# Value half of the last up projection as seven block products for 16 channel tiles

## The chip, the core and the metric

The kernel runs on one core of a Trainium2 chip. What counts is the device time of one execution in microseconds (us). The engines are TensorE (PE), VectorE (DVE), ScalarE (ACT), GpSimd (POOL) and the DMA queues, which SyncE (SP) and ScalarE issue here. SBUF is the on-chip memory, PSUM the accumulators of TensorE, HBM the memory outside.

## The reference

Two layers of an encoder over 256 tokens, width 2048, with 16 learned tokens put in front and dropped at the end:

```python
h = RMSNorm(x)
[q | k | v | f | ga | gf] = h @ W_in
a = attention(q, k, v) @ W_attn_br      # 8 heads, 2 key heads, RMSNorm and rotary on q and k
s = fourier(f) @ W_four                 # Re of a 2-D DFT per channel group
x = x + (sigmoid(ga) * a + sigmoid(gf) * s) @ W_out
h2 = RMSNorm(x)
u = dwconv3(h2 @ W_up_gate)             # taps over positions t-1, t, t+1
x = x + (silu(u) * (h2 @ W_up_val)) @ W_down
```

All is float32. W_up has 2 x 5632 columns: 44 channel tiles of 128 for the gate half and 44 for the value half. The tokens that count in the last layer's value half are 256, two halves of 128.

## The kernel before

**Precision by splitting.** A float32 product is made of three faster ones: each operand is a sum of a high part (a cast to F32R) and a low part (what the cast left), and hi x hi, hi x lo and lo x hi are added in PSUM. Activations are kept so in xHL. Weights come in chunks of 128 x 1024 floats (512 KB): load_raw has SyncE load a chunk (tile raw, four buffers), split_w has ScalarE cast it (wh, line 233, three buffers) and VectorE subtract (wl, line 236). A chunk is 4 k-tiles for 2 channel tiles (MG = 2), and a product over 2048 inputs for two channel tiles is a group of four chunks.

**The order of the work.** The list order, written at the start, names every group and its chunks: mix of a layer (k, v, q, then per half ga, gf, s, a and eight o groups), then the up and down groups. advance keeps loads ahead of use, and the splitting of a chunk is put into the queues LOOK = 2 chunks ahead of its matmuls. Engines take their instructions in the order in which the program issues them. Everything that isn't a weight's split or a matmul hangs between matmuls: generators are pushed with a delay onto a list (shadow), and step(), called after every second k-tile and channel tile, lets one of them go on; drain() runs all that are left at once. A second list (behindhand) holds generators with steps of their own. Folded weights for the Fourier group (fold_w, line 219) use the tile wpm, two buffers, instead of a split.

**Seven products.** In the last layer the down projection of the first 36 channel tiles is made by a scheme with seven block products in place of eight (PRODUCTS): inputs and weights are taken as 2 x 2 blocks, each product multiplies a sum of input blocks by a sum of weight blocks, and results are added into four output blocks (C4). weight_sums makes the four sums of weight blocks needed, on VectorE in layer 0's feed-forward stage, with loads and stores on ScalarE's queue, and stores them in HBM (tsum); later they come as chunks like any weight. The products of one up block's channels run in between the next up block's groups (FF_SPLIT gives the blocks of 22, 14 and 8 channel tiles); combos makes the sums of inputs, block_ the matmuls (line 1043), 512 wide.

**The last up projection.** For each pair of channel tiles a gate group (ug, three matmuls of 258 columns per k-tile and channel tile) is followed by a value group (uv). In the value groups one matmul of 512 columns takes the high weight against both parts of x, and one of 256 the low weight (lines 303, 304). On the gate u is scaled by rstdB, which holds 1/rms for every token, then come the taps (lines 1105, 1107, 1108) and Silu (1109); the product with rstdB (1110) and with the value gives g. The first part of norm_stats (1/rms) is made while the first gate group runs, and drain() is called after that group.

## Time and profile before

| what | us |
|---|---|
| time, median of 3 runs (lowest to highest) | 2509.56 (2509.33 to 2509.77) |
| the profiled execution | 2509.57 |
| its span, from the first to the last instruction | 2507.6 |
| TensorE busy | 2500.3 |
| VectorE busy | 1800.7 |
| ScalarE busy | 1255.1 |
| GpSimd busy | 18.2 |

A row of the groups gives the line, the engine, the operation with the tiles that it writes and reads, shapes and count; then the busy time and the mean in ns of one; then how long the engine was idle just before these instructions, and what ended that wait. A row of the timeline is the start, the length, and the same names, with a wait ahead of it in brackets.

### The profile page before, as it was taken

How to read it: one execution, taken by the hardware profiler on the slowest of the kernel's cores; microseconds unless marked ns; L12 is line 12 of the kernel's file. 1: busy time of each engine (PE TensorE's matmuls, PEld its weight loads, DVE VectorE, ACT ScalarE, POOL GpSimd, SP SyncE). 2: the span in 40 equal slices, each digit the busy share in tenths (PEclk: the TensorE clock that was granted, in tenths of full speed). 3: DMA queues.
4: the chain of work that ended last, by engine and by line, in shares of the span. 5: the costliest groups of instructions: out<-in, count | busy, mean ns of one | idle time of the engine just before them, and what ended most of it. 6: DMA issues, size and time to landing. Idle time of an engine off the chain costs nothing.

```text
span 2507.6 us, 47695 instructions
## 1 busy us (share of the span) xinstructions
PE 2500.3 (100%) x19334; PEld 2432.0 (97%) x19334; DVE 1800.7 (72%) x2717; ACT 1255.1 (50%) x1862; POOL 18.2 (1%) x37
## 2 busy tenths in 40 slices
PE   9999999999999999999999999999999999999999
PEld 9999999999999999999999999999999998888888
DVE  7687666777777557777655887666766668888986
ACT  6455334454454334544444564444544556666663
POOL 0000000000000000000000000000000000000000
PEclk9999999999999999999999999999999999999999
DMA  7545555568888888888754546565555567888885
GB/s 241 167 157 173 184 186 198 178 205 297 281 295 291 286 297 287 288 294 289 252 177 155 178 157 206 188 203 195 192 187 192 187 220 266 267 265 267 268 268 192
DMA packets 160524, 569.15 MB, mean 227 GB/s; under 512 B 18480, under 2 KB 22320, under 8 KB 160304
## 3 DMA queue, kind: packets, MB, share of 16 engines
q1 hardware_dynamic: 135200, 485.69, 58.0%
q10 hardware_dynamic: 25104, 80.43, 9.3%
q8 instruction: 151, 2.47, 0.4%
q14 instruction: 69, 0.57, 0.1%
HBM read 523.41 MB, written 39.85 MB: 225 GB/s over the span
## 4 chain that ended last, share of the span: by engine, by line
PE 98%; DVE 1%; DMA 0%; ACT 0%; issue 0%; SPq 0%; ACTq 0%; DVEq 0%
PE ps_x L1043 7%; PE ps_ug L307 7%; PE ps_ug L309 7%; PE ps_ug L308 7%; PE ps_uv L303 6%; PE ps_d L309 4%; PE ps_d L307 4%; PE ps_d L308 3%; PE ps_uv L307 3%; PE ps_uv L309 3%; PE ps_uv L308 3%; PE ps_uv L304 3%; PE ps_o L307 2%; PE ps_gf L307 2%; PE ps_gf L309 2%; PE ps_s L339 2%
## 5 line engine op out<-in xcount | busy, mean ns | idle before, releaser
L236 DVE TENSOR_TENSOR wl<-raw,wh 128x1024 fp32r<-128x1024 f32 (+1 forms) x889 | 1083.2, 1220 | 555.4 <-ACT wh L233 550.5
L233 ACT CAST wh<-raw 128x1024 fp32r<-128x1024 f32 (+1 forms) x888 | 928.9, 1046 | 929.9 <-PE ps_ug L308 212.7
L307 PE MATMUL ps_ug<-xHL,wh 128*128 128x272 f32 (+1 forms) x1408 | 398.8, 283 | 0.0
L309 PE MATMUL ps_ug<-xHL,wl 128*128 128x272 f32 (+1 forms) x1408 | 397.1, 282 | 0.0
L308 PE MATMUL ps_ug<-xHL,wh 128*128 128x272 f32 (+1 forms) x1408 | 396.8, 282 | 0.0
L307 PEld LDWEIGHTS ps_ug<-xHL,wh 128*128 128x128 f32 x1408 | 264.3, 188 | 2.2
L308 PEld LDWEIGHTS ps_ug<-xHL,wh 128*128 128x128 f32 x1408 | 264.6, 188 | 1.9
L309 PEld LDWEIGHTS ps_ug<-xHL,wl 128*128 128x128 f32 x1408 | 264.4, 188 | 0.0
L303 PE MATMUL ps_uv<-xHL,wh 128*128 128x512 f32 x704 | 247.1, 391 | 0.0
L307 PE MATMUL ps_d<-gHL,wh 128*128 128x272 f32 (+1 forms) x720 | 205.8, 286 | 0.0
L309 PE MATMUL ps_d<-gHL,wl 128*128 128x272 f32 (+1 forms) x720 | 205.2, 285 | 0.0
L308 PE MATMUL ps_d<-gHL,wh 128*128 128x272 f32 (+1 forms) x720 | 204.4, 284 | 0.0
L307 PE MATMUL ps_uv<-xHL,wh 128*128 128x272 f32 x704 | 201.3, 286 | 0.0
L309 PE MATMUL ps_uv<-xHL,wl 128*128 128x272 f32 x704 | 200.6, 285 | 0.0
L308 PE MATMUL ps_uv<-xHL,wh 128*128 128x272 f32 x704 | 199.9, 284 | 0.0
L304 PE MATMUL ps_uv<-xHL,wl 128*128 128x256 f32 x704 | 198.2, 282 | 0.0
L1043 PE MATMUL ps_x<-wh,cb 128*128 128x512 f32 x504 | 171.0, 392 | 0.0
L303 PEld LDWEIGHTS ps_uv<-xHL,wh 128*128 128x128 f32 x704 | 132.0, 188 | 28.0
L307 PE MATMUL ps_ga<-xHL,wh 128*128 128x272 f32 (+1 forms) x512 | 146.9, 287 | 0.0
L307 PE MATMUL ps_gf<-xHL,wh 128*128 128x272 f32 (+1 forms) x512 | 145.7, 285 | 0.0
L307 PE MATMUL ps_o<-mH,wh 128*128 128x272 f32 (+1 forms) x512 | 144.6, 282 | 0.0
L309 PE MATMUL ps_ga<-xHL,wl 128*128 128x272 f32 (+1 forms) x512 | 144.6, 282 | 0.0
(287 smaller groups left out, 5738.7 us busy)
## 6 DMA issues: line engine op xcount, KB each, us to landing
raw<-in_w_up SPq DMA_DIRECT2D x352, 512.0 KB, 4.4
raw<-in_w_in SPq DMA_DIRECT2D x206, 512.0 KB, 3.6
raw<-in_w_down SPq DMA_DIRECT2D x104, 512.0 KB, 4.5
b<-in_w_blk ACTq DMA_DIRECT2D x72, 512.0 KB, 5.0
ts<-b ACTq DMA_DIRECT2D x72, 512.0 KB, 5.3
raw<-ts SPq DMA_DIRECT2D x72, 512.0 KB, 4.5
raw<-in_w_out SPq DMA_DIRECT2D x64, 512.0 KB, 3.5
raw<-in_w_blk SPq DMA_DIRECT2D x54, 512.0 KB, 4.5
```

What stands on the lines that cost most here:

```text
L233: nc.scalar.copy(h[:, a:b], r[:, a:b])
L236: nc.vector.tensor_tensor(lo[:, a:b], r[:, a:b], h[:, a:b].bitcast(F32), op=ALU.subtract)
L303: nc.tensor.matmul(o2, h[:, c, sl], ab, start=kt == 0, stop=False)
L304: nc.tensor.matmul(o, lo[:, c, sl], ab[:, 0, :], start=False, stop=kt == nk - 1)
L307: nc.tensor.matmul(o, h[:, c, sl], a, start=kt == 0, stop=False)
L308: nc.tensor.matmul(o, h[:, c, sl], b, start=False, stop=False)
L309: nc.tensor.matmul(o, lo[:, c, sl], a, start=False, stop=kt == nk - 1)
L339: nc.tensor.matmul(ps[e][:, :TH], ws[j][:, 2 * e + c, sl], fr[:, kt, e], start=kt == 0, stop=e == 1 and kt == 3)
L1043: nc.tensor.matmul(ps[e], cb[:, s_, q - q4], w, start=q == 0 and a == 0 and p in (1, 2, 7), stop=q == n - 1 and a == 2, skip_group_check=True)
```

## The change

The value half of the first 16 channel tiles of the last layer (VG = 2 groups of VT = 8) is no longer made by uv groups. For each group of eight tiles, x (256 tokens x 2048) and the weights (2048 x 1024) are taken as 2 x 2 blocks, and seven products of 128 tokens x 1024 x 512 are made, tokens on the output's partitions. Their 56 chunks (512 KB, two k-tiles of 512 columns) are spread between the gate groups of the first up block, from six chunks into it; each chunk is six matmuls, 512 wide.

- **Inputs.** forms() makes normed x times the norm's weight in float32 (16 scaled copies into C4), and the four sums of its blocks with their high and low parts (tile F). It is pushed with a delay of 14 steps ahead of the first gate group.
- **Weights.** Three products take blocks as they are (w_val, a new layout of the same weights), four take sums (vsum, in HBM). There are eight sets of sums. Two (VEARLY) are made by weight_sums in layer 0, which starts after 8 steps instead of 24. Six are made by late_sums in the last layer's mix stage, each as two halves of 512 columns: four loads, four subtractions or additions, four stores, in the two buffers of wpm. late_sums pauses while the branch groups (ga, gf, s, a) run; settle() ends the half that is open when a branch begins, and what is left when the feed-forward stage begins is issued at once.
- **Results.** vgather adds a product, scaled by 1/rms of its tokens, into the blocks in C4. values() transposes them to channels on partitions and multiplies them into the gates, which are stored without rstdB for these tiles.
- **Blocks.** FF_SPLIT is 24, 12, 8 in place of 22, 14, 8.

```diff
...
-FF_SPLIT = ((24, 20), (22, 14, 8))
+FF_SPLIT = ((24, 20), (24, 12, 8))
 NPR = sum(FF_SPLIT[-1][:2]) // 2
 PRODUCTS = ((1, "11"), (2, "11"), (6, "21"), (7, "22"), (5, "22"), (4, "21"), (3, "12"))
+VG, VT, VEARLY = 2, 8, 2
...
+    vsum = [[dram.tile([P, D // 2], F32, name=f"vs{q}_{e}") for e in range(4)] for q in range(4 * VG)]
...
+                if l < DEPTH - 1 or MG * i >= VT * VG:
+                    ups.append(((l, "uv", i), g(w_up, FT // MG + i, 0, KT)))
...
+                a0, a1 = (6, 4) if c == 0 else (2 if c == 1 else 0, 0)
+                if c == 0:
+                    for v in range(VG):
+                        for p, _ in PRODUCTS:
+                            for q in range(4):
+                                src = {1: w_val[v, 0, 0, q], 2: w_val[v, 1, 0, q], 3: w_val[v, 1, 1, q],
+                                       5: vsum[4 * v + q][0], 7: vsum[4 * v + q][1], 6: vsum[4 * v + q][2], 4: vsum[4 * v + q][3]}[p]
+                                xs_.append((src.rearrange("p (c m) -> p c m", c=CW), ("v", v, p, q)))
+                for p, _ in PRODUCTS if c else ():
                     for q in range(FF_SPLIT[l][c - 1] // 2):
...
-                slots = sum(len(chs) for _, chs in ups)
-                at = done = 0
+                slots = sum(len(chs) for _, chs in ups) - a0 - a1
+                at, done = -a0, 0
...
-        for s in list(behindhand):
+        for s in list(behindhand) if not st.get("branch") else ():
...
+    def settle():
+        while st.get("open"):
+            s = behindhand[-1]
+            s[0] = next(s[1])
...
+    parked = [([w_blk[2 * q + e // 2, e % 2] for e in range(4)], tsum[q]) for q in range(NPR)]
+    vparked = [([w_val[q // 4, e // 2, e % 2, q % 4] for e in range(4)], vsum[q]) for q in range(4 * VG)]
+    parked, vparked = parked + vparked[:VEARLY], [([t_[:, a:a + 512] for t_ in f], [t_[:, a:a + 512] for t_ in to]) for f, to in vparked[VEARLY:] for a in (0, 512)]
+
+    def late_sums():
+        for src, dst in vparked:
+            while st.get("branch"):
+                yield 1
+            st["open"] = True
+            ab = [wp.tile([P, CW, MG * P], F32, tag="wpm", name=f"sum{i}", bufs=2).rearrange("p c m -> p (c m)") for i in range(2)]
+            b = {0: ab[0][:, :512], 1: ab[0][:, 512:], 3: ab[1][:, :512], 2: ab[1][:, 512:]}
+            for e in (0, 1, 3, 2):
+                nc.scalar.copy(b[e][:, 0:1], st["cur"][:, 0, 0:1].bitcast(F32))
+                nc.scalar.dma_start(b[e], src[e])
+                yield 2
+            yield 4
+            one = small.tile([P, 32], F32, tag="one", name="one", bufs=2)[:, 0:1]
+            nc.scalar.activation(one, st["new"][:, 0, 0:1].bitcast(F32), AF.Identity, bias=1.0, scale=0.0)
+            for o, x, y, to in ((0, 1, 0, 0), (1, 3, 1, 1), (3, 3, 0, 2), (2, 2, 3, 3)):
+                nc.vector.scalar_tensor_tensor(b[o], b[x], one, b[y], op0=ALU.mult, op1=ALU.subtract)
+                yield 2
+                nc.scalar.dma_start(dst[to], b[o])
+            st["open"] = False
+            yield 4
...
+        if last:
+            behindhand.append([60, late_sums()])
...
+                settle()
+                st["branch"] = True
...
+                st["branch"] = False
...
+        while behindhand:
+            step(True)
...
+                while c == 0 and prods["vals"] < VG:
+                    yield 1
...
+            def forms():
+                xg = C4.rearrange("p a (k t) -> p (a k) t", t=SEQ)
+                for k in range(KT):
+                    nc.scalar.activation(xg[:, k], XT[:, k, NM:T], AF.Copy, scale=prm[:, P_NF + l * KT + k:P_NF + l * KT + k + 1])
+                    yield 1
+                f = [fp.tile([P, 2, 2, 8, P], F32R, tag=t, name="F") for t in ("g1", "cb")]
+                fm = {7: f[0][:, 0], 5: f[0][:, 1], 6: f[1][:, 0], 3: f[1][:, 1]}
+                tt = nc.vector.tensor_tensor
+                for k in (0, 4):
+                    A = {f"{h + 1}{j + 1}": xg[:, 8 * j + k:8 * j + k + 4, P * h:P * h + P] for h in range(2) for j in range(2)}
+
+                    def put(p, x):
+                        o = fm[p][:, :, k:k + 4]
+                        nc.scalar.copy(o[:, 0], x)
+                        tt(o[:, 1], x, o[:, 0].bitcast(F32), op=ALU.subtract)
+
+                    x, y = (fp.tile([P, 4, P], F32, tag="sx", name="sx", bufs=2) for _ in range(2))
+                    tt(x, A["21"], A["22"], op=ALU.add)
+                    put(5, x)
+                    yield 1
+                    tt(y, A["11"], A["21"], op=ALU.subtract)
+                    put(7, y)
+                    yield 1
+                    tt(x, x, A["11"], op=ALU.subtract)
+                    put(6, x)
+                    yield 1
+                    tt(x, A["12"], x, op=ALU.subtract)
+                    put(3, x)
+                    yield 1
+                prods["forms"] = fm
+
+            def vgather(v, p, ps):
+                to = dict(PRODUCTS)[p]
+                by = hold["tok"][:, int(to[0]):int(to[0]) + 1]
+                o = C4[:, 2 * int(to[0]) + int(to[1]) - 3, 512 * (v % 2):512 * (v % 2) + 512]
+                if p in (1, 6, 7, 3):
+                    nc.scalar.activation(o, ps, AF.Identity, scale=by)
+                else:
+                    nc.vector.scalar_tensor_tensor(o, ps, by, o, op0=ALU.mult, op1=ALU.add)
+                yield 1
+
+            def values(v):
+                for i in range(0, VT, 2):
+                    while prods["gates"] < VT * v + i + 2:
+                        yield 1
+                    pt = psum.tile([P, 512], F32, tag="aux", name="ps_vv")
+                    for m in range(2):
+                        for hh in range(2):
+                            at = 512 * (v % 2) + (i + m) % 4 * P
+                            nc.tensor.transpose(pt[:, P * (2 * m + hh):P * (2 * m + hh) + P], C4[:, 2 * hh + (i + m) // 4, at:at + P], ident)
+                    x = sets[0][:, VT * v + i:VT * v + i + 2, :]
+                    nc.vector.tensor_tensor(x, x, pt.rearrange("p (m t) -> p m t", m=2), op=ALU.mult)
+                    yield 1
+                prods["vals"] = v + 1
+
+            def vblock(key, h, lo):
+                _, v, p, q = key
+                while p not in (1, 2, 4) and "forms" not in prods:
+                    step(True)
+                row = 0 if p in (1, 6, 5, 3) else 1
+                if p == row + 1 and q == 0:
+                    prods[row] = psum.tile([P, 512], F32, tag="aux", name=f"ps_y{v}{p}")
...
+                ps = prods[row]
+                for kk in range(2):
+                    kt = 2 * q + kk
+                    if p in (1, 2, 4):
+                        k, t0 = {1: (kt, NM), 2: (8 + kt, NM), 4: (8 + kt, NM + P)}[p]
+                        a = [xHL[:, k, r, X_AT[l][r] + t0:X_AT[l][r] + t0 + P] for r in range(2)]
+                    else:
+                        a = [prods["forms"][p][:, r, kt] for r in range(2)]
+                    wh, wl = (t_.rearrange("p c m -> p (c m)")[:, 512 * kk:512 * kk + 512] for t_ in (h, lo))
+                    for n, (s_, w) in enumerate(((a[0], wh), (a[0], wl), (a[1], wh))):
+                        nc.tensor.matmul(ps, s_, w, start=kt == 0 and n == 0 and p in (1, 2, 7), stop=kt == 7 and n == 2, skip_group_check=True)
+                    step()
+                    pump()
+                if q == 3:
+                    prods["out"]["v", v, p] = vgather(v, p, ps)
+                    push(prods["out"]["v", v, p], 1)
+                    if p == 3:
+                        push(values(v), 6)
...
-                behindhand.append([24, weight_sums()])
+                behindhand.append([8, weight_sums(parked)])
...
+                if last and c == 0:
+                    push(forms(), 14)
...
+                        if last and mt < VT * VG:
+                            nc.scalar.activation(sets[0][:, mt, :], cv[:, lo2:T], AF.Silu)
+                            prods["gates"] = mt + 1
+                            continue
...
+                    if not cs:
+                        continue
...
```

**Places in the order.** Names carry the number of the chunk behind wh, wl, raw and wpm; what stands in brackets are the queues that an instruction waits for.

VectorE at the start of the last up projection, before. ug_0 (chunks 600 to 603) is the first gate group, u and cv its gate:

```order
L236 TENSOR_TENSOR wl605_21919<-raw605_21754,wh605_21918 128x1024 [waits DMAHW2_49,PE_49,Activation_49]
L1103 TENSOR_TENSOR u_21945<-ps_1_ug_0_0_21803,rstdB_149 128x258 [waits Activation_49]
L1103 TENSOR_TENSOR u_21953<-ps_1_ug_0_1_21804,rstdB_149 128x258 [waits PE_49]
L1107 SCALAR_TENSOR_TENSOR cv_21947<-u_21945,prm_142,cv_21947 128x256 [waits Activation_49]
L1108 SCALAR_TENSOR_TENSOR cv_21947<-u_21945,prm_142,cv_21947 128x255 [waits DVE_49]
L236 TENSOR_TENSOR wl606_21970<-raw606_21805,wh606_21969 128x1024 [waits DMAHW3_49,Activation_49]
```

and with the change, where sum is a half sum of late_sums, sx and F belong to forms():

```order
L554 SCALAR_TENSOR_TENSOR sum0_22101<-sum1_22102,one_22111,sum0_22101 128x512 [waits DMAHW7_49,DVE_49]
L247 TENSOR_TENSOR wl605_22243<-raw605_22048,wh605_22242 128x1024 [waits PE_49,Activation_49]
L554 SCALAR_TENSOR_TENSOR sum1_22102<-sum1_22102,one_22111,sum0_22101 128x512 [waits DMAHW3_49,DMAHW2_49,DVE_49]
L1245 TENSOR_TENSOR u_22315<-ps_1_ug_0_0_22127,rstdB_181 128x258 [waits Activation_49]
L554 SCALAR_TENSOR_TENSOR sum1_22102<-sum1_22102,one_22111 128x512 [waits DMAHW0_49,DVE_49]
L1245 TENSOR_TENSOR u_22322<-ps_1_ug_0_1_22128,rstdB_181 128x258 [waits PE_49]
L1097 TENSOR_TENSOR sx_22287<-C4_22124 128x512 [waits Activation_49]
L1100 TENSOR_TENSOR sx_22288<-C4_22124 128x512
L1094 TENSOR_TENSOR F_22285<-sx_22287,F_22285 128x512 [waits Activation_49]
L1094 TENSOR_TENSOR F_22285<-sx_22288,F_22285 128x512 [waits Activation_49]
...
L1094 TENSOR_TENSOR F_22286<-sx_22301,F_22286 128x512 [waits Activation_49]
L247 TENSOR_TENSOR wl606_22340<-raw606_22129,wh606_22339 128x1024 [waits DMAHW1_49]
```

Between wl605 and wl606 stand 24 instructions, which were four: the last half sum's two remaining subtractions, the gate's, and the eight combinations and eight low parts of forms().

ScalarE over the same stretch, before:

```order
L233 CAST wh603_21843<-raw603_21680 128x1024 [waits DMAHW0_49,PE_49]
L233 CAST wh604_21884<-raw604_21724 128x1024 [waits DMAHW1_49,PE_49,Activation_49]
L233 CAST wh605_21918<-raw605_21754 128x1024 [waits DMAHW2_49,DVE_49,PE_49]
L514 COPY rstdB_149<-ps_nb_21928 128x272 [waits PE_49]
L1105 ACTIVATE cv_21947<-u_21945,prm_142 128x256 [waits DVE_49]
L233 CAST wh606_21969<-raw606_21805 128x1024 [waits DMAHW3_49,PE_49,Activation_49]
```

and with the change (vs7 is the eighth set of sums in HBM, in_w_val the weights that are loaded for the twelfth half sum):

```order
L556 DMA vs7_2_159<-sum1_21965 128x512 [waits DMAHW2_49,DVE_49]
L556 DMA vs7_3_160<-sum1_21965 128x512 [waits DVE_49]
...
L547 COPY sum0_22101<-wh599_21976 128x1
...
L548 DMA sum0_22101<-in_w_val 128x512 [waits DMAHW5_49,Activation_49]
...
L547 COPY sum1_22102<-wh599_21976 128x1 [waits DMAHW3_49,DMAHW2_49]
...
L244 CAST wh604_22208<-raw604_22016 128x1024 [waits PE_49]
L548 DMA sum1_22102<-in_w_val 128x512 [waits Activation_49] x2
L244 CAST wh605_22242<-raw605_22048 128x1024
...
L556 DMA vs7_2_159<-sum1_22102 128x512 [waits DMAHW5_49,DVE_49]
...
L556 DMA vs7_3_160<-sum1_22102 128x512 [waits DMAHW6_49,DVE_49]
L1083 ACTIVATE C4_22124<-XT_170,prm_174 128x256 x9
L1093 CAST F_22285<-sx_22287 128x512 [waits DVE_49]
```

The stores of the eleventh half sum, the loads and stores of the twelfth and the last nine scaled copies stand around the casts of chunks 604 and 605, in the same queue.

VectorE at the start of the second half's branches, before; wpm544 and wpm545 are the first folded Fourier weights, chunks 542 and 543 the last of the first half's o groups:

```order
L219 TENSOR_TENSOR wpm544_19915<-raw544_19779 128x512 [waits DMAHW4_49]
...
L219 TENSOR_TENSOR wpm544_19915<-raw544_19779 128x512
L236 TENSOR_TENSOR wl542_19852<-raw542_19715,wh542_19851 128x1024 [waits DMAHW2_49,Activation_49]
L219 TENSOR_TENSOR wpm545_19944<-raw545_19809 128x512 [waits DMAHW5_49]
L219 TENSOR_TENSOR wpm545_19944<-raw545_19809 128x512
L236 TENSOR_TENSOR wl543_19882<-raw543_19745,wh543_19881 128x1024 [waits DMAHW3_49,PE_49,Activation_49]
```

and with the change:

```order
L554 SCALAR_TENSOR_TENSOR sum0_20097<-sum0_20097,one_20199 128x512 [waits DMAHW6_49,DMAHW1_49,DMAHW7_49,DMAHW0_49,Activation_49]
L554 SCALAR_TENSOR_TENSOR sum0_20097<-sum1_20098,one_20199,sum0_20097 128x512 [waits DMAHW0_49,DVE_49]
L247 TENSOR_TENSOR wl546_20218<-raw546_20067,wh546_20217 128x1024 [waits DMAHW1_49,Activation_49]
L554 SCALAR_TENSOR_TENSOR sum1_20098<-sum1_20098,one_20199,sum0_20097 128x512 [waits DMAHW4_49,DMAHW3_49,DVE_49]
L554 SCALAR_TENSOR_TENSOR sum1_20098<-sum1_20098,one_20199 128x512 [waits DMAHW2_49,DVE_49]
...
L230 TENSOR_TENSOR wpm544_20147<-raw544_19996 128x512 [waits DMAHW5_49,DMAHW4_49]
L230 TENSOR_TENSOR wpm544_20147<-raw544_19996 128x512
...
L247 TENSOR_TENSOR wl547_20245<-raw547_20101,wh547_20244 128x1024 [waits DMAHW3_49,Activation_49]
L230 TENSOR_TENSOR wpm545_20178<-raw545_20030 128x512 [waits DMAHW7_49,DMAHW0_49,DVE_49]
L230 TENSOR_TENSOR wpm545_20178<-raw545_20030 128x512
```

The folds stood ahead of wl542 and wl543; now they stand behind a half sum's four instructions, and behind wl546 and wl547, and wait for more queues.

36 lines of the change are left out of this document (22 added, 14 removed).

## The prediction

> **What bounds the kernel now.** I read the page's first part and its chain of waits, then the groups of the two engines that feed TensorE.
>
> ```profile
> span 2507.6 us, 47695 instructions
> PE 2500.3 (100%) x19334; PEld 2432.0 (97%) x19334; DVE 1800.7 (72%) x2717; ACT 1255.1 (50%) x1862; POOL 18.2 (1%) x37
> ...
> PE 98%; DVE 1%; DMA 0%; ACT 0%; issue 0%; SPq 0%; ACTq 0%; DVEq 0%
> ```
>
> PE is busy for the whole span and is 98% of the chain that ended last. So a matmul less is time saved, and any time in which PE has no weights is time lost: there is no slack to absorb it. Weights reach PE in chunks of 128x1024: ScalarE casts the high half, VectorE subtracts for the low half.
>
> ```profile
> L236 DVE TENSOR_TENSOR wl<-raw,wh 128x1024 fp32r<-128x1024 f32 x884 | 1080.4, 1224 | 555.0 <-ACT wh L233 550.1 <-issue 0.3
> L233 ACT CAST wh<-raw 128x1024 fp32r<-128x1024 f32 x884 | 926.7, 1049 | 929.7 <-PE ps_ug L308 212.7 <-PE ps_d L308 130.5 <-issue 81.6
> ```
>
> The casts wait for PE, because three buffers hold wh: cast i starts when PE is through chunk i-3. The lead over PE is then the PE time of two chunks, less 1.05 + 1.22 us for the two halves. VectorE and ScalarE take their instructions in order, so anything queued ahead of a cast or a subtraction that together exceeds this lead stops PE. All terms below are made against the profiled execution: 2509.57 us, of which 2.0 lie around the span. It is within 0.01 of the runs' median, 2509.56.
>
> **What PE saves.** Three forms price it: the fused value pair (512 and 256 wide), the block product's 512-wide matmul, and four transposes.
>
> ```profile
> 1809.80 0.39 PE L303 MATMUL ps_uv<-xHL,wh 128*128 128x512 f32 x1
> 1810.03 0.28 PE L304 MATMUL ps_uv<-xHL,wl 128*128 128x256 f32 x1
> 1810.15 0.39 PE L303 MATMUL ps_uv<-xHL,wh 128*128 128x512 f32 x1
> ...
> 2456.34 0.39 PE L1043 MATMUL ps_x<-wl,cb 128*128 128x512 f32 x1
> 2456.56 0.39 PE L1043 MATMUL ps_x<-wh,cb 128*128 128x512 f32 x1
> 2456.79 0.39 PE L303 MATMUL ps_d<-gHL,wh 128*128 128x512 f32 x1
> ...
> 2458.18 0.60 PE L1058 MATMUL ps_ct<-cst,C 128*128 128x128 f32 x4
> 2458.53 0.48 PE L303 MATMUL ps_d<-gHL,wh 128*128 128x512 f32 x1
> 2458.85 0.28 PE L304 MATMUL ps_d<-gHL,wl 128*128 128x256 f32 x1
> 2458.97 0.39 PE L303 MATMUL ps_d<-gHL,wh 128*128 128x512 f32 x1
> 2459.20 0.28 PE L304 MATMUL ps_d<-gHL,wl 128*128 128x256 f32 x1
> 2459.32 0.60 PE L1058 MATMUL ps_ct<-cst,C 128*128 128x128 f32 x4
> ```
>
> Start to start, a pair takes 1810.15 - 1809.80 = 0.35 (0.347 over longer stretches), a 512-wide product 0.22 to 0.23 (I use 0.23), four transposes 1.14 - 2 x 0.347 = 0.45. Removed: 16 tiles x 16 k-tiles = 256 pairs, 88.9 us. Added: 7 products x 2 groups x 4 chunks x 6 = 336 matmuls, 77.3 us, and 8 sets of four transposes, 3.6 us. The down projection's split moves from 22, 14 to 24, 12 tiles, still 18 pairs of blocks. **Net on PE: -8.0 us.**
>
> **Work that has cover.** Two sums move into layer 0's sums, which end inside that stage by order. The other six become 12 halves in layer 1's mix stage, each with four loads and four stores of 256 KB; in the up stage 56 chunks take the place of 32.
>
> ```profile
> 1745.00:1790.00 45.00, 45.00 (x391) 45.00 (x391) 38.36 (x66) 27.89 (x47) 0.00 (x0) 1.00 0.56 187
> 1790.00:2037.00 247.00, 247.00 (x1781) 232.89 (x1780) 166.04 (x237) 123.82 (x164) 0.85 (x1) 1.00 0.57 189
> 2037.00:2300.00 263.00, 263.00 (x1576) 233.96 (x1575) 214.23 (x262) 166.25 (x202) 0.00 (x0) 1.00 0.80 264
> ```
>
> These rows are stretches of layer 1: the end of its mix stage, its first up block (where the new products go), and the next, where block products already run. After the length come PE, PEld, VectorE and ScalarE busy, then clock, DMA share and GB/s. The next block lives with VectorE at 214/263 = 81% and DMA at 0.80 without a gap on PE; the first block, at 67%, has room for 24 more chunks' halves, the scalings and the multiplies. Transfers: 12 x 2 MB over some 445 us of mix is 54 GB/s on top of 187, under the 264 that left PE whole. I cost both at nothing; if the cover failed, the 24 chunks alone are 24 x 1.22 = 29 us of VectorE. The second block's gates take the memory of F; its last reader, product 3 of the second group, is followed by four more up chunks (11 us), so I cost that at nothing too. The costs lie where queues bunch.
>
> **Junction into the last up stage.** Here the order puts 24 VectorE instructions between wl605 and wl606 where four stood. Before, this stretch ran so (PE, VectorE, ScalarE):
>
> ```profile
> 1801.71 0.28 PE L309 MATMUL ps_ug<-xHL,wl 128*128 128x258 f32 x1
> 1801.83 0.39 PE L303 MATMUL ps_uv<-xHL,wh 128*128 128x512 f32 x1
> ...
> 1799.75 1.23 DVE L236 TENSOR_TENSOR wl<-raw,wh 128x1024 fp32r<-128x1024 f32 x1
> ...
> 1803.28 1.22 DVE L236 TENSOR_TENSOR wl<-raw,wh 128x1024 fp32r<-128x1024 f32 x1
> ...
> 1802.01 1.04 ACT L233 CAST wh<-raw 128x1024 fp32r<-128x1024 f32 x1
> ```
>
> The first gate group ends at 1801.83; wl605 starts at 1799.75 and wl606 at 1803.28. In the new kernel two chunks of the second gate group (2.78 us each) lie between that end and chunk 606, whose low half PE takes 0.24 us into it: it must be there at 1801.83 + 5.55 + 0.24 = 1807.6. The new instructions are of these kinds:
>
> ```profile
> L1012 DVE TENSOR_TENSOR cb<-sx,cb 128x512 fp32r<-128x512 f32 x12 | 8.2, 685 | 0.0
> L1002 DVE TENSOR_TENSOR sx<-g 128x512 f32<-128x512 f32 x9 | 6.2, 689 | 0.1
> L1011 ACT CAST cb<-sx 128x512 fp32r<-128x512 f32 x12 | 7.4, 614 | 0.0
> L1103 DVE TENSOR_TENSOR u<-ps_ug,rstdB 128x258 f32<-128x258 f32 x44 | 18.0, 422 | 3.5 <-PE ps_ug L309 3.4
> L1107 DVE SCALAR_TENSOR_TENSOR cv<-u,prm,cv 128x256 f32<-128x256 f32 x44 | 20.5, 481 | 0.3 <-ACT cv L1105 0.2
> ```
>
> **The floor**: were every input ready, the eight combinations and eight low halves take 16 x 0.61 (0.685 busy, of which 0.07 overlaps the next one: the two folds quoted below take 1.30 together), the last gate tile's u and four taps with the same overlap 0.35 + 4 x 0.41, and wl606 itself 1.22: 13.0 us from 1801.83 to 1814.8, **7.2 late**. But inputs aren't ready, since the last half sum is forced out just ahead, and it is a chain across the queues: store the 11th sum's results, wait till they land (the buffer is the same), issue the loads behind that wait, cast wh604 behind it too, wait for the loads, subtract twice on VectorE with wl605 between, and only then ScalarE issues the last stores, and behind these makes nine of the 16 scaled copies of x which the combinations read. How long 256 KB takes is not in the trace; its neighbours are
>
> ```profile
> raw<-in_w_out SPq DMA_DIRECT2D x64, 512.0 KB, 3.5
> outT<-ot ACTq DMA_DIRECT2D x16, 128.0 KB, 2.1
> ts<-b ACTq DMA_DIRECT2D x72, 512.0 KB, 5.3
> L479 ACT ACTIVATE xHL<-XT,prm 128x272 fp32r<-128x272 f32 x64 | 32.2, 519 | 43.0 <-DVE XT L947 26.2 <-DVE XT L1151 13.6 <-DMA XT<-in_xT 2.6
> ```
>
> so 2.1 to 5.3, and I take about 3 (halfway from 128 KB to 512 KB at this stage's load). From the 11th sum's last subtraction at 1794.5 (behind wl602): stored 1798, wh604 cast 1799.3, loads landed 1802.8, wl605 done 1803.1, last subtraction 1804.9, nine copies at 0.41 until 1809, then combination, cast and subtraction alternate between the engines (16 x 0.65, the two gate activations and taps between) to wl606's end at 1821.4: 13.9 late. Each us more per transfer counts twice (2.1 us: 12.1 late; 5.3: 18.5), and an 11th sum that is itself late by its loads adds 2 to 4. Between the floor of 7.2 and 20, **I take 16**, the walk with half of that lateness. Behind wl606 the whole of the first products' chunks queue up, and only PE waits for them.
>
> **Start of the second branch half.** The folded Fourier weights wpm544 and wpm545 share the sums' two buffers and now come behind a sum's stores and behind wl546 and wl547; before, they were folded ahead of wl542 and wl543. The next subtractions and PE's first Fourier group stand behind them.
>
> ```profile
> 1539.99 1.30 DVE L219 TENSOR_TENSOR wpm<-raw 128x512 f32<-128x512 f32 x2
> ```
>
> A store that lands in about 3 us behind four subtractions (4 x 0.685) and then 1.30 per fold, less the lead of two chunks (5.5): at best 0, at worst, with a 5.3 us store, 5. **I take 3.5.**
>
> **Sums among the attention's queues.** Five half sums lie in the projection and attention part; a ScalarE store there waits for a subtraction that waits for a load, and a cast (wh475) stands behind four such. Each wait of up to 5.3 us is set against a lead of 3.3 (5.55 - 1.05 - 1.22): 0 to 2 each, five times; **I take 3** of 0 to 8.
>
> **Clock after the long gap.**
>
> ```profile
> 4.48 0.71 PE L361 MATMUL ps_f<-xHL,wh 128*128 128x272 f32 x2
> ...
> 6.56 0.29 PE L360 MATMUL ps_f<-xHL,wh 128*128 128x272 f32 x1
> 6.68 0.28 PE L361 MATMUL ps_f<-xHL,wh 128*128 128x272 f32 x1
> ...
> 14.22 0.39 PE L360 MATMUL ps_f<-xHL,wh 128*128 128x272 f32 x1 [1.11 <-ACT wh L233]
> 14.45 0.29 PE L361 MATMUL ps_f<-xHL,wh 128*128 128x272 f32 x1
> ```
>
> At the program's start two matmuls take 0.71 where from 6.6 us on they start every 0.12; a gap of 1.11 us later costs no such slowness. A gap of 16 us is like the start: the 5.2 us from there (1.05, PE's first row, to 6.2) at half pace bound it at 2.6, and nothing bounds it below. **I take 1.5.** The Trainium skill, "TensorE: Matmul & The Clock Gate", Part 1, halves the clock after an idle window of about 3.4 us and restores it after about 3.4 us of work; by its figures the loss would be an estimated 1.7 for each gap longer than that, which makes 2525.7 with the junction alone and 2527.4 with the folds' gap, and the trace of before has no long gap in mid program to test it.
>
> **Sum**: -8.0 + 16 + 3.5 + 3 + 1.5 = +16.0; 2509.57 + 16.0 = **2525.5 us**.
>
> **Rivals.** *Only the burst* is paid: the forced sum is done before PE reaches the gate group, the folds and the attention absorb theirs. Then 2509.6 - 8.0 + 7.2 = 2508.8: not slower, and this decides from the point where the copies of x are done by 1801.8, 7 us earlier than in my walk. For it: casts and subtractions idle for 930 and 555 us in total. Against: the store waits in the order can't be passed, and the landing times above are measured. *Everything hidden*: the gap at the junction doesn't arise as PE finds earlier work, 2509.6 - 8.0 = 2501.6, faster. This decides from the point where all 24 instructions fit in 5.8 us; they are 11.8 by their rows. *The sums clog more*: each of 12 half sums costs its store or load wait (2 us beyond the lead) wherever it is, 24 in place of my 6.5 for two of the places: 2543. *Nothing gained on PE*, if products into one accumulator don't keep the 0.23 spacing: at 0.25, 336 x 0.02 = 7 more, 2532.
>
> **How the numbers follow.** What a measurement can tell from no change is about 0.2%, 5 us. The forecast with its neighbours (2515 to 2538) gets 0.68; the burst alone 0.12, within 0.2%; all hidden 0.05, faster; clogging 0.10 and slow products 0.05, slower. So faster 0.05, same 0.12, slower 0.83. The junction's own bounds give 2517 (with 7.2) to 2530 (with 20). With the other terms at their ends too, the walk at its shortest transfers gives 2509.6 - 8.0 + 12.1 = 2514, and the upper ends 2509.6 - 8.0 + 20 + 5 + 8 + 2.6 = 2537. The range, 2511 to 2541, takes in these and a part of the clogging.
>
> **What would show it.** Right: one PE gap of over 10 us before chunk 606, ended by VectorE's wl, with F and sx ahead of it; gaps of some us at the second half's folds ended by DMA or VectorE; products 0.23 apart; matmuls slower for some us after the long gap. Wrong: no gap at the junction above 7, or gaps spread over the first up block (VectorE short there after all), or in layer 0.

## The result

The changed kernel takes 2548.83 us (median of 5 runs, 2547.28 to 2553.76), the kernel before 2509.77 beside it (2509.33 to 2510.61): slower by 1.6%, ratio 1.016 with a 95% interval of 1.0145 to 1.0175. Forecast were 2525.5 in a range of 2511 to 2541: the sign is right, the size was missed by 23 us, and the time lies above the range.

The profiled execution took 2552.70 us, so it is to be held against the 2509.57 of before. The first two rows of its page:

```profile
span 2550.8 us, 47905 instructions
PE 2508.9 (98%) x19190; PEld 2425.6 (95%) x19190; DVE 1867.1 (73%) x2779; ACT 1297.9 (51%) x1976; POOL 18.2 (1%) x37
```

TensorE runs 144 matmuls fewer, and is busy 8.6 us longer: busy time includes matmuls at a lower clock. To find the place I take, in both traces, the start of the first matmul of each stage (for the second half's branches that of the last o matmul, so that the wait for the first folds counts with them); the table has the length of each stage.

| stage | before, us | changed, us | difference |
|---|---|---|---|
| up to layer 0's first up group | 521.3 | 522.2 | +0.9 |
| layer 0's feed-forward | 775.2 | 775.2 | 0.0 |
| layer 1's first projections, attention begins | 130.3 | 140.5 | +10.2 |
| branches of the first half | 169.3 | 176.4 | +7.1 |
| o groups of the first half | 44.3 | 44.3 | 0.0 |
| branches of the second half | 105.1 | 111.0 | +5.9 |
| o groups of the second half | 44.4 | 44.4 | 0.0 |
| last up blocks, to the last down groups | 666.9 | 685.9 | +19.0 |
| last down groups | 47.3 | 47.3 | 0.0 |

The differences add up to 43.1 us, the whole of 2552.70 - 2509.57. A second split of the same sum: gaps between matmuls (start-to-start distance over the usual one of the form by more than 0.15 us) are 47.4 us in all, 6.3 before. That is +41.1; the arithmetic saved 8.1 (below); 10.1 are left, of which matmuls at a lower clock account for 6.6 (see Clock).

**Attention.** The groups of waits from layer 1's start to the junction (engine, line, what it waited for; us in total, times, longest):

```profile
ACT sum L547 <- DMA vs<-sum: 22.9, 11, 3.5
ACT wh L244 <- DVE sum L554: 4.5, 1, 4.5
ACT wh L244 <- DMA vs<-sum: 4.0, 1, 4.0
...
ACT wh L244 <- DMA sum<-in_w_val: 2.2, 1, 2.2
```

By these rows ScalarE stood 33.6 us for the half sums: for the stores of one to land before it touched the buffer for the next, and for loads and subtractions. Not all of it cost TensorE time: 14.0 lie in attention (7.3 for stores in three waits, 4.5, 2.2), the rest in the stages behind it, where the o groups lost nothing. One such place, ScalarE's and then TensorE's timeline:

```profile
1413.28 0.29 ACT L547 COPY sum<-wh 128x1 f32<-128x1 f32 x2 [3.36 <-DMA vs<-sum]
1413.50 0.82 ACTq L548 DMA_DIRECT2D sum<-in_w_val  x2
1414.42 2.50 ACTq L722 DMA_DIRECT2D qs<-qp  x4
1416.96 1.04 ACT L244 CAST wh<-raw 128x1024 fp32r<-128x1024 f32 x1 [3.39 <-DVE rq L836]
...
1415.72 0.28 PE L325 MATMUL ps_q<-xHL,wl 128*128 128x258 f32 x1
1418.05 0.39 PE L323 MATMUL ps_q<-xHL,wh 128*128 128x258 f32 x1 [2.05 <-ACT wh L244]
```

The copy waits 3.36 us for a store, attention's own four transfers come behind it, the cast of the next weights behind these, and TensorE stands 2.05 us for that cast. The wait of 4.5 us is another cast, which stands behind four of attention's transfers (2.46 us to issue) and a store that waits for its subtraction:

```profile
1383.87 1.05 ACT L244 CAST wh<-raw 128x1024 fp32r<-128x1024 f32 x1 [4.54 <-DVE sum L554]
```

256 KB took nearly as long to land (the last figure, a median in us) as the 5.0 and 5.3 that 512 KB took on the same queue before, in layer 0:

```profile
sum<-in_w_val ACTq DMA_DIRECT2D x48, 256.0 KB, 4.7
vs<-sum ACTq DMA_DIRECT2D x48, 256.0 KB, 5.0
```

**Second half.** TensorE waits for the folded weights, as forecast, in two gaps:

```profile
1661.51 3.73 PE L355 MATMUL ps_s<-fr,wpm 128*128 128x138 f32 x16 [2.66 <-DVE wpm L230]
1666.45 0.74 PE L355 MATMUL ps_s<-fr,wpm 128*128 128x138 f32 x4 [1.22 <-DVE wpm L230]
```

**Junction.** ScalarE, VectorE and TensorE at the start of the last up stage:

```profile
1826.58 0.28 ACT L547 COPY sum<-wh 128x1 f32<-128x1 f32 x2 [3.50 <-DMA vs<-sum]
...
1834.70 2.30 ACTq L556 DMA_DIRECT2D vs<-sum  x1
1837.04 3.69 ACT L1083 ACTIVATE C<-XT,prm 128x256 f32<-128x256 f32 x9 [2.46 <-issue]
...
1839.18 0.69 DVE L1097 TENSOR_TENSOR sx<-C 128x512 f32<-128x512 f32 x1 [4.17 <-ACT C L1083]
1851.29 3.49 DVE L247 TENSOR_TENSOR wl<-raw,wh 128x1024 fp32r<-128x1024 f32 x3
...
1843.75 0.58 PE L323 MATMUL ps_ug<-xHL,wh 128*128 128x258 f32 x1 [8.04 <-ACT wh L244]
1845.73 0.79 PE L1155 MATMUL ps_y<-wh,xHL 128*128 128x512 f32 x1 [0.76 <-ACT wh L244]
1852.57 0.80 PE L325 MATMUL ps_ug<-xHL,wl 128*128 128x258 f32 x2 [6.04 <-DVE wl L247]
```

The order is that of the walk: the copy for the last half sum waits for a store (3.50), its own stores follow, the nine scaled copies come behind them at 1837, the combinations start at 1839.18, and wl606 starts at 1851.29. TensorE stands 8.04 us for wh606, which is behind the copies and casts of the forms, and 6.04 for wl606. So it isn't one gap ended by wl606, as the prediction expected to see, but two, and the longer one is ended by the cast. With smaller ones before, the gaps between 1824 and 1853 are 19.7 us.

**Clock.** Stretches of 5 us of the changed kernel (length, then busy PE, PEld, VectorE, ScalarE, POOL, granted clock, DMA share, GB/s):

```profile
1420.00:1425.00 5.00, 4.39 (x24) 4.18 (x24) 3.70 (x5) 3.57 (x8) 0.00 (x0) 0.68 0.53 178
1455.00:1460.00 5.00, 4.07 (x24) 4.07 (x25) 4.95 (x12) 2.06 (x5) 0.00 (x0) 0.74 0.42 126
1660.00:1665.00 5.00, 3.49 (x16) 3.33 (x16) 3.53 (x6) 0.99 (x2) 0.00 (x0) 0.72 0.98 277
1850.00:1855.00 5.00, 2.43 (x11) 2.44 (x12) 4.78 (x6) 0.75 (x2) 0.00 (x0) 0.50 0.29 94
1839.65:1856.71 17.06, 6.17 (x24) 5.37 (x25) 14.33 (x23) 11.07 (x19) 0.00 (x0) 0.50 0.17 50
```

Four times, not once, the granted clock falls to a half: three times for 3.4 us and, at the junction, for 17.1 (last row), of which TensorE is busy 6.17. The matmuls that start in these stretches, gaps aside, lost 1.5, 1.5, 1.1 and 2.5 us by start-to-start distance: 6.6 of the 10.1. The other 3.5 aren't shown to be clock. In the run with both edits (below) the clock never fell, and the same sum leaves 2.3 us there: -3.5 in all is 2.3 of gaps, 8.1 saved and 2.3 more.

### The profile page after: what moved, and what is told of

It reads as the page before. It is cut to its first block, busy times and chain, and to the rows that moved or that the text cites. A ratio compares the mean times of both kernels' runs of the same rounds, so it can differ in the third digit from the quotient of the medians.

```text
span 2550.8 us, 47905 instructions
## 1 busy us (share of the span) xinstructions
PE 2508.9 (98%) x19190; PEld 2425.6 (95%) x19190; DVE 1867.1 (73%) x2779; ACT 1297.9 (51%) x1976; POOL 18.2 (1%) x37
## 3 DMA queue, kind: packets, MB, share of 16 engines
q8 instruction: 150, 2.46, 0.4%
## 5 line engine op out<-in xcount | busy, mean ns | idle before, releaser
L247 DVE TENSOR_TENSOR wl<-raw,wh 128x1024 fp32r<-128x1024 f32 (+1 forms) x913 | 1112.1, 1220 | 512.0 <-ACT wh L244 507.2
L244 ACT CAST wh<-raw 128x1024 fp32r<-128x1024 f32 (+1 forms) x912 | 953.0, 1046 | 889.0 <-PE ps_ug L324 188.4
L319 PE MATMUL ps_uv<-xHL,wh 128*128 128x512 f32 x448 | 158.6, 392 | 0.0
L323 PE MATMUL ps_ga<-xHL,wh 128*128 128x272 f32 (+1 forms) x512 | 146.9, 287 | 0.5 <-ACT wh L244 0.5
L324 PE MATMUL ps_ga<-xHL,wh 128*128 128x272 f32 (+1 forms) x512 | 144.6, 283 | 0.0
L325 PE MATMUL ps_gf<-xHL,wl 128*128 128x272 f32 (+1 forms) x512 | 144.4, 282 | 0.0
```

The source lines that it names most:

```text
L244: nc.scalar.copy(h[:, a:b], r[:, a:b])
L247: nc.vector.tensor_tensor(lo[:, a:b], r[:, a:b], h[:, a:b].bitcast(F32), op=ALU.subtract)
L319: nc.tensor.matmul(o2, h[:, c, sl], ab, start=kt == 0, stop=False)
L323: nc.tensor.matmul(o, h[:, c, sl], a, start=kt == 0, stop=False)
L324: nc.tensor.matmul(o, h[:, c, sl], b, start=False, stop=False)
L325: nc.tensor.matmul(o, lo[:, c, sl], a, start=False, stop=kt == nk - 1)
```

## The experiments

First the stages of all runs with a change of order, as differences to the profiled execution before, in us (the last up blocks hold TensorE's saving):

| run | to layer 0's up | first projections | branches 1 | o groups 1 | branches 2 | o groups 2 | last up blocks | sum |
|---|---|---|---|---|---|---|---|---|
| the change | +0.9 | +10.2 | +7.1 | 0.0 | +5.9 | 0.0 | +19.0 | +43.1 |
| no late half sums | -0.3 | -0.1 | 0.0 | 0.0 | 0.0 | 0.0 | +1.2 | +0.9 |
| forms spread | -0.3 | +13.2 | +8.1 | +1.1 | +6.4 | 0.0 | +9.1 | +37.6 |
| both | -0.6 | 0.0 | 0.0 | 0.0 | 0.0 | 0.0 | -2.9 | -3.5 |
| half sums in o groups | +8.2 | +0.5 | 0.0 | +1.3 | +5.4 | +10.5 | -0.8 | +25.1 |
| on SyncE's queue | -1.0 | +5.0 | +1.6 | 0.0 | +7.8 | 0.0 | +7.1 | +20.5 |
| SyncE, slow, spread | -0.7 | +2.0 | 0.0 | 0.0 | +0.6 | 0.0 | -2.9 | -1.0 |
| ScalarE, slow, spread | +0.6 | +4.3 | -0.5 | 0.0 | +0.3 | +0.2 | -1.9 | +3.1 |
| SyncE, ahead of q | +0.3 | -0.2 | +0.1 | 0.0 | 0.0 | 0.0 | -2.7 | -2.6 |
| the same, blocks 22, 14, 8 | -0.4 | 0.0 | +0.1 | 0.0 | 0.0 | 0.0 | -1.9 | -2.3 |

### Without the late half sums

```diff
+                                if 4 * v + q >= VEARLY and p in (4, 5, 6, 7):
+                                    src = w_val[v, p % 2, p // 6, q]
...
-        if last:
-            behindhand.append([60, late_sums()])
```

> The changed kernel without the twelve late half sums: the products whose weight sums were made late read unsummed blocks of the same size, so their values are wrong and nothing else differs. Theory (the late sums' waits in the queues of ScalarE and VectorE cost the mix stage its 23.2 us and push the scaled copies back at the junction): the mix stage takes its old time within 1 us, the junction keeps the burst of the input forms with 7 to 10 us of gap and 2 to 4 us of slow clock, total 2510 to 2517. Rival (the burst alone makes the whole gap of some 20 us, the sums only stand beside it): mix stage as of old, total 2520 to 2524. Rival (the mix stage is slowed by something else, the two more early sums for example): mix stage still over 15 us longer, total over 2530.

Measured: 2510.48 us, ratio 1.0003 (0.9993 to 1.0012). The mix stage has its old time to 0.1 us, so the twelve half sums cost 38 of the 39 us, with all that their waits set off. What the burst of the forms costs by itself is one gap, in TensorE's timeline of this run:

```profile
1812.40 0.59 PE L327 MATMUL ps_ug<-xHL,wl 128*128 128x258 f32 x2 [4.46 <-DVE wl L249]
```

My 7 to 10 us for it were too many: with no stores ahead of them the scaled copies are early, and the first combination starts at 1798.83, ahead of the first gate group's end, and not behind it (VectorE's timeline):

```profile
1798.83 0.69 DVE L1097 TENSOR_TENSOR sx<-C 128x512 f32<-128x512 f32 x1 [0.18 <-ACT C L1083]
```

### The forms spread

```diff
-                if last and c == 0:
-                    push(forms(), 14)
...
                     if i == 0:
                         drain()
+                        if last:
+                            push(forms(), 2)
...
+                while "forms" not in prods:
+                    yield 1
```

> The changed kernel with one edit: the input forms are started after the first gate group's drain, one piece per step, instead of ahead of it, so that the drain no longer issues them all at once. Theory: the two gaps of 8.2 and 6.6 us go, and the slow clock behind them; what is left at the junction are the 3 to 5 us of the last forced half sum; total 2529 to 2535. Rival (the burst only moves, to the first products that read the forms): gap of 7 us or more a few chunks later, total over 2540.

Measured: 2548.86 us, ratio 1.0155 (1.014 to 1.017): no gain in the time, against the theory and nearer to the rival, whose gap of 7 us doesn't come either (the longest below is 3.30). The last up stage is 9.9 us shorter than in the change's profile, but the first combinations still wait behind the last half sum's stores, and gaps are left at the first products (TensorE's timeline of this run):

```profile
1845.09 0.50 PE L1157 MATMUL ps_y<-wh,xHL 128*128 128x512 f32 x1 [1.39 <-ACT wh L244]
1846.35 0.80 PE L1157 MATMUL ps_y<-wl,xHL 128*128 128x512 f32 x1 [0.76 <-DVE wl L247]
1861.54 0.51 PE L325 MATMUL ps_ug<-xHL,wl 128*128 128x258 f32 x2 [3.30 <-DVE wl L247]
```

The mix stage took 28.8 us more than before in this execution, and 23.2 in the change's, though VectorE's order in it is the same to the instruction. A chain that hangs on landings may vary with them, which may also be why the change's runs lie 6.5 us apart and those of before 1.3; neither was tried.

### Both

> Both edits: no late half sums (values wrong for the products that read unsummed blocks) and the forms spread. Theory: what is left is the gain on TensorE, -8.0 us, and next to no gap: 2501 to 2505. Rival (the first up block is short of VectorE or of DMA with 24 more chunks): 2508 to 2515 with gaps all over that block.

Measured: 2506.24 us, ratio 0.9989 (0.9979 to 0.9999), between the theory and the rival. This is the ceiling: what the products save when no late sum is made at all. The gain on TensorE is there, but only 2.9 us of it arrive. By start-to-start distances the 336 products take 78.1 us (0.232 each) and the 32 transposes 2.8, where 256 pairs took 89.0 (244.7 us for 704): 8.1 saved. Given back are four gaps of 0.5 to 0.9 us and small ones below them: the gate's 2112 matmuls take 250.8 us start to start where they took 247.7, the 896 left in the value groups 157.9 where 89.0 less than 244.7 would be 155.7.

### Half sums in the o groups

The changed kernel lost nothing in the o groups, so all twelve went there, 19 steps apart where they had been 24, the forms spread.

```diff
-            while st.get("branch"):
+            while st.get("o", 0) <= 0:
                 yield 1
+            st["o"] -= 1
...
-                yield 2
-            yield 4
+                yield 1
+            yield 5
...
+                st["o"] = 3
                 for mg in range(8):
...
+                st["o"] = 0
+                settle()
```

> The forms spread, and all twelve half sums made, but only while output projection groups run: three in each of the four (two layers, two halves), ended two or three chunks ahead of the next stage. Outputs as the reference wants them. Theory (a half sum costs only where attention or a stage's end is short of queue time; in the output projection's stretches the changed kernel lost 0.00 us with seven sums in them): 2501 to 2506. Rival (every half sum costs its wait wherever it is, about 2 us): 2520 or more. Rival (layer 0's stretches, 272 wide, or the starts of the branches behind them still lose a few us): 2507 to 2515.

Measured: 2535.02 us, ratio 1.010 (1.0085 to 1.0115). Theory and place fall: layer 0 now loses 8.2 us, 7.4 of them in its second stretch of o groups, and layer 1's second stretch 10.5. The time is that of the first rival (2520 or more), but not its 2 us for each half sum wherever it is: the first stretches lose 0.0 and 1.3, and the branches behind them 1.4 and 5.4. ScalarE, then TensorE, near the end of layer 0's second stretch:

```profile
515.25 0.28 ACT L548 COPY sum<-wh 128x1 f32<-128x1 f32 x2 [4.25 <-DMA vs<-sum]
516.38 1.04 ACT L244 CAST wh<-raw 128x1024 fp32r<-128x1024 f32 x1 [0.85 <-DMA raw<-in_w_up]
...
517.48 0.59 PE L323 MATMUL ps_o<-mH,wh 128*128 128x272 f32 x1 [3.68 <-ACT wh L244]
```

The same wait for a store's landing, with less time between one half sum's stores and the next one's loads. It isn't the stage alone that decides, but how far apart the halves are, and what stands behind the wait. That left two candidates, the queue and the pace.

### On SyncE's queue

```diff
-                nc.scalar.copy(b[e][:, 0:1], st["cur"][:, 0, 0:1].bitcast(F32))
-                nc.scalar.dma_start(b[e], src[e])
+                nc.sync.dma_start(b[e], src[e])
...
-                nc.scalar.dma_start(dst[to], b[o])
+                nc.sync.dma_start(dst[to], b[o])
```

> The changed kernel with one edit: the late half sums' loads and stores go out on SyncE's queue and no ScalarE copy holds them back; order, pace, buffers and the burst of the forms stay. Theory (ScalarE, taking its queue in order, waits for the sums' stores to land and for their subtractions, with the casts behind): the mix stage's extra 23 us fall below 8, the junction keeps the burst, 8 to 12 us of gap with slow clock; total 2511 to 2522. Rival (VectorE's subtractions waiting for the loads hold wl back, whatever queue issues them): the mix stage stays 15 us or more longer, total over 2530. Rival (SyncE's weight loads now wait behind the stores and come late): gaps ended by DMA raw, total over 2530.

Measured: 2527.98 us, ratio 1.0072 (1.0057 to 1.0088). The move gives back 20.8 us. It changes more than the queue, though. No copy holds the loads back now, so that they go out earlier (the first half sum's from 466.6 us, still in layer 0). And the order of attention's own instructions is another: in layer 1's first projections and first branches, leaving out those of the sums, 58 of VectorE's 434 stand elsewhere in the changed kernel than before, 28 in this run, and none or one in the runs that lost next to nothing there (no late sums, half sums in the o groups, ahead of the q groups). What that order costs by itself, no run shows. In the mix stage 14.4 of 23.2 remain, 7.8 of them at the second half's start. There VectorE's subtractions wait for loads, and the folds for stores; VectorE, then TensorE:

```profile
1643.34 0.75 DVE L553 SCALAR_TENSOR_TENSOR sum<-sum,one 128x512 f32<-128x512 f32 x1 [2.18 <-DMA sum<-in_w_val]
1650.17 1.29 DVE L230 TENSOR_TENSOR wpm<-raw 128x512 f32<-128x512 f32 x2 [0.90 <-DMA vs<-sum]
...
1650.92 1.29 PE L355 MATMUL ps_s<-fr,wpm 128*128 128x138 f32 x4 [4.67 <-DVE wpm L230]
```

and the last forced half sum holds the norm's VectorE work at the junction, since tok and dg stand behind a subtraction that waits:

```profile
1816.39 0.75 DVE L553 SCALAR_TENSOR_TENSOR sum<-sum,one 128x512 f32<-128x512 f32 x1 [2.77 <-DMA sum<-in_w_val]
...
1817.82 1.25 PE L529 MATMUL ps_nb<-dg,ones 128*128 128x272 f32 x2 [2.75 <-DVE tok L532]
1832.09 0.80 PE L325 MATMUL ps_ug<-xHL,wl 128*128 128x258 f32 x2 [4.46 <-DVE wl L247]
```

So about half went with ScalarE's queue; the rest is halves that begin too late to end ahead of the next stage, and the burst. The theory's total (up to 2522) was too low, the rivals' too high.

### Slow pace, with either queue

Two half sums in each of the four stretches of o groups and four in layer 1's first projections, 32 steps apart, none open when a branch or the feed-forward begins; the forms spread. Beside the edits of the run in the o groups:

```diff
-                yield 1
-            yield 5
+                yield 2
+            yield 8
...
-            yield 2
+            yield 8
...
+        else:
+            st["o"] = 4
...
+                st["o"] = 0
+                settle()
...
-                st["o"] = 3
+                st["o"] = 2
```

> All half sums made, outputs as the reference wants them: on SyncE's queue as in the run beside it, four steps apart in place of two to six, two per output projection half in both layers and four in the last layer's first projections, none open when a branch or the feed-forward stage begins, and the forms spread. Theory: mix stages within 2 us of old, up stages as without late sums (about 3 us less than before): 2505 to 2509. Rival (the subtractions of 12 half sums still cost their waits): 2515 or more.

> The same as the run on SyncE's queue with the slow pace, but loads and stores on ScalarE's queue with the copies that hold them back, as in the changed kernel. If the pace alone decides: 2505 to 2510. If the waits in ScalarE's queue decide: 10 us or more above the run on SyncE's queue, with gaps ended by casts (wh) that stood behind a store's landing.

Measured: on SyncE's queue 2508.66 us, ratio 0.9997 (0.9988 to 1.0006); on ScalarE's 2513.05, ratio 1.0012 (1.0003 to 1.0021). The first is as its theory had it, the second between its two. At this pace and in these places the queue is worth some 4 us. On ScalarE's queue, with the forms spread in both, the old pace and places took 2548.86, 35.8 us more: the pace, the places, and that nothing is forced at a stage's end, do most; which of them does how much was not tried apart. ScalarE's waits for a store's landing fall from 22.9 us in 11 (above) to 0.8 in one. What is left is a gap among the q groups, ended by a wl that stands behind a wait for attention's own transfer; ScalarE's waits, VectorE's and TensorE's timeline of that run:

```profile
ACT sum L548 <- DMA vs<-sum: 0.8, 1, 0.8
...
1401.77 0.73 DVE L730 TENSOR_TENSOR qs<-qs,cst 128x544 f32<-128x544 f32 x1 [3.02 <-DMA qs<-qp]
...
1405.08 0.39 PE L325 MATMUL ps_q<-xHL,wl 128*128 128x258 f32 x1 [2.83 <-DVE wl L247]
```

### Bursts in the kernel before

```diff
+                    if last and c == 0:
+                        for _ in range({2: 8, 4: 10, 6: 12, 8: 16, 10: 24}.get(i, 0)):
+                            nc.vector.tensor_tensor(C4[:, 0, :512], XT[:, 0:2, NM:T], XT[:, 2:4, NM:T], op=ALU.add)
```

> The kernel before with five bursts of VectorE additions (128x512, results unused) ahead of gate tiles of the last layer's first up block: 8, 10, 12, 16 and 24 of them, at 0.61 us each 4.9, 6.1, 7.3, 9.8 and 14.6 us. By a lead of 3.3 us the gaps on TensorE are about 1.6, 2.8, 4, 6.5 and 11.3 us, 26 in all: 2536 with nothing else. If the clock falls after gaps over 3 us and costs some 1.7 each: 2541, granted clock of 0.5 right behind the last three. If it falls after every gap over 2 us: behind the last four, 2543. If it doesn't fall: 2536.

Measured: 2510.6 us in the one run, and no gap in that block. The additions depend on nothing in that stage, and the order of instructions put all 70 of them early, one by one into VectorE's idle time, as the row of the tile shows:

```profile
L1099 DVE TENSOR_TENSOR C<-XT x70: 680/687/695, 1791.9 to 1908.7; 128x512 f32<-128x512 f32 x70
```

70 x 0.687 = 48 us of VectorE in 117 us of the first up block cost nothing. On the clock the run says nothing; the gaps of the other runs do (last section).

### Ahead of the q groups, and the old blocks

The four half sums in layer 1's first projections 24 steps apart, so that they end ahead of q; then the same with the up blocks of before.

```diff
-            yield 8
+            yield st.get("pace", 8)
...
-            st["o"] = 4
+            st["o"], st["pace"] = 4, 4
...
-FF_SPLIT = ((24, 20), (24, 12, 8))
+FF_SPLIT = ((24, 20), (22, 14, 8))
```

> The kernel of the slow pace on SyncE's queue with one edit: the four half sums of the last layer's first projections are 24 steps apart and not 32, so that the last is through ahead of the q groups, where that kernel had two gaps of 1 us each among attention's work. Theory (a half sum costs nothing where ScalarE and VectorE have no attention work between the weight halves): the first projections take their old time within 0.5 us instead of 2.0 more, total 2505.5 to 2508. Rival (the shorter distance makes VectorE wait for loads): 2509 or more.

> The same with the up blocks of before, 22, 14 and 8 channel tiles instead of 24, 12 and 8. In the second block the products of the first then run between 14 tiles' groups, not 12. Theory (the few gaps of 0.5 to 0.9 us that remain in the last up stage come from the tighter second block): 1 to 2 us less than the run beside it, 2504 to 2507. Rival (the first block gets tighter instead, 56 value chunks between fewer groups): the same or 1 to 3 us more.

Measured: 2507.88 us, ratio 0.9995 (0.9986 to 1.0004), and 2507.89, ratio 0.9993 (0.9984 to 1.0002). In the first, layer 1's whole mix stage is back at its old time, with all sums made; layer 0's loses 1.2 us in its second half's branches, which the first column hides, since the kernel's start varies by as much. The groups of their subtractions (busy, mean ns, idle before) and their transfers show why:

```profile
L554 DVE SCALAR_TENSOR_TENSOR sum<-sum,one,sum 128x512 f32<-128x512 f32 x24 | 17.9, 747 | 0.2
L554 DVE SCALAR_TENSOR_TENSOR sum<-sum,one 128x512 f32<-128x512 f32 x24 | 17.9, 747 | 0.2
...
sum<-in_w_val SPq DMA_DIRECT2D x48, 256.0 KB, 5.2
vs<-sum SPq DMA_DIRECT2D x48, 256.0 KB, 4.5
```

The transfers land no sooner than in the changed kernel, but nothing waits long for them. VectorE's 0.4 us in all were 2.5 in the changed kernel and 5.6 in the run on SyncE's queue, and ScalarE's queue holds none of them. The loads go out earlier, too: those of the fifth half sum, which is subtracted in layer 1 at 1305, are issued at 518.8 us, still in layer 0. The theory on the first projections holds (-0.2). The blocks make no difference: the theory on the second block falls. Both lie 1.6 us below before, inside what can be measured; no kernel here is shown to beat it, and the ceiling is 3 us.

## Why the prediction was wrong

- **What bounds the kernel** (right): gaps on TensorE, its saving and its clock account for 39.6 of the 43.1 us.
- **What PE saves** (right): -8.0 forecast, -8.1 by distances.
- **Work that has cover** (half right): the 24 more chunks cost no 29 us of VectorE, and the early sums nothing; but in the last up stage about 5 of the 8 us saved don't arrive even with no burst and no sums, where I had put nothing.
- **Junction** (right in the chain, 3.7 us short): 16 forecast, 19.7 of gaps. The walk had wl606 come last; the longer gap, 8.04, is ended by wh606, whose cast stands behind the copies and casts of the forms. My floor of 7.2 was no floor: alone the burst costs a gap of 4.5, since the combinations may begin before the gate group ends.
- **Second half's start** (right in mechanism): 3.5 forecast; 4.6 of gaps there, 5.9 in all.
- **Sums among the attention's queues**: this step failed. I took 3 of at most 8, and it was 12.8 us of gaps and 17.3 in all. I had let five half sums cost 0 to 2 us each, as a wait less a lead of 3.3 us, and counted one wait for each. But several stand in a row in ScalarE's queue: the copies wait for the last half sum's stores to land, attention's own four transfers follow with 2.5 us of issue, a store waits for its subtraction, and then come the casts, which had stood 4.54 us at 1383.87 and 3.39 at 1416.96. Each is over the lead, and as I read it the lead isn't there again when the next wait comes. VectorE itself idled only 1.0 us there for the sums' loads. The landing itself was mis-sized too: I took about 3 us for 256 KB between 2.1 and 5.3, and it was 4.7 and 5.0. The move to SyncE's queue fits this: first projections and first branches fall from 17.3 to 6.6 with the same instructions on VectorE. But their order changed with it, so how much was the waits and how much the order stays open.
- **Clock after the long gap**: 1.5 forecast, 6.6 measured. I reckoned with one long gap. That stretch cost 2.5; the other 4.1 came behind gaps of 2 to 3 us in attention and at the second half's start, to which I had given no clock at all.
- **Rivals**: the nearest was that the sums clog more, 2543, with a chance of 0.10. Its time came within 6 us of the measured one, by luck: its mechanism was not right. A half sum doesn't cost its wait wherever it is, since the four that were begun and ended while o groups ran cost 0.0. Slow products didn't occur (0.232 us each).

By terms, forecast against measured: -8.0 / -8.1, junction 16 / 19.7, second half 3.5 / 4.6, attention 3 / 12.8, clock 1.5 / 6.6. The last two hold 14.9 of the 27.1 us between +16.0 and the profiled run's +43.1; the rest is the junction's 3.7, the folds' 1.1, 4 us of small gaps elsewhere, 2.4 of them in the second up block, and 3.5 us that are neither gaps over 0.15 us nor clock.

## What to carry to other kernels

Before a transfer is issued from an engine that also feeds the bottleneck, list what that engine has to wait for ahead of the issue (the last use of the buffer, landed), and what stands behind it: here 12 x 8 small transfers cost 38 us on ScalarE's queue at a quick pace, some 7 there at a slow one in better places, and under 2 on SyncE's, spread out and clear of the q groups (2513.05 and 2507.88 against the ceiling's 2506.24). Work that fills idle time must be ended early, not forced at the end of a stage. Where gaps of 2 us or more arise on TensorE, reckon with the clock on top: a slow stretch of 3.4 us cost 1.1 to 1.7 us in these runs.
